# Part of the two down products of a macaron block computed by seven products of sums

## The chip, the cores and the metric

The kernel runs on one core of a Trainium2 chip. The metric is the device time of one execution in microseconds. Engines: TensorE (PE; PEld its weight load), VectorE (DVE), ScalarE (ACT), GpSimd (POOL), and SyncE (SP), whose queue issues loads. Matmuls accumulate into PSUM banks of 512 fp32 columns.

## What is computed

512 token rows of width 1024 pass through a feed-forward block, a token mixer (windowed attention and a gated recurrence), and a second feed-forward block. Each of the three has a residual with a factor and a layer norm behind it:

```python
def swiglu(x, w1, w3, w2):
    return (jax.nn.silu(x @ w1) * (x @ w3)) @ w2

x = layer_norm(DEEPNORM_ALPHA * x + 0.5 * swiglu(x, ffn1_w1[l], ffn1_w3[l], ffn1_w2[l]), ln1_g[l], ln1_b[l])
mix = token_mixer(x, ...)
x = layer_norm(DEEPNORM_ALPHA * x + mix, ln2_g[l], ln2_b[l])
x = layer_norm(DEEPNORM_ALPHA * x + 0.5 * swiglu(x, ffn2_w1[l], ffn2_w3[l], ffn2_w2[l]), ln3_g[l], ln3_b[l])
```

The hidden width is 2816, that is 22 feature tiles of 128. All is fp32.

## The kernel before

Every fp32 operand of a matmul is split into a high part (a cast to fp32r on ACT, line 74) and a low part (the difference, on DVE, line 75), by the helper `split`. A product is three matmuls: high by high, and the two mixed ones (lines 106 to 108). Weights come in blocks of 128 x 1024: SP's queue loads one into a raw buffer (`raw`, line 79, five buffers), and `wsplit` puts its two parts into a ring of four.

The up products of a feed-forward block already are done by seven products of sums of blocks (Strassen's scheme in Winograd's form) for all but the first pair of feature tiles: class `Quads`, whose matmuls are line 282 and whose sums of weights are line 297. Their operands, mixtures of the input's four blocks, lie in eight slots x0 to x7, named by `OPS` in the order in which the products use them. The gated results, g[0] to g[10], each a pair of feature tiles for all 512 tokens, stay in SBUF as g0 to g10; line 512 is the last multiplication that forms one.

The down product is `down_and_norm`. For each output half of 512 columns (dh = 0, 1) it goes through 22 feature tiles in eleven weight slabs; for every feature tile four row tiles of 128 tokens are multiplied, the last as two pieces of 256 columns. `lhs(k)` gives the two parts of a feature tile and splits them at first need, into the slots x0 to x7, into tiles of the pool `dn`, or into g4 and g5. The residual rows are loaded into g0 to g3 behind the first half's matmuls (`get_res`, line 549, on ACT's queue) and take the sums by `drain` (line 466). In the second half the last six feature tiles go row by row, so that the layer norm of a row tile runs beside the matmuls of the next.

The pool `up` (sums, gates) is closed before the pool `dn` is opened, and both lie on the same side of SBUF. The order of the instructions on each engine comes from a planner that runs when the kernel is built: it takes what is written first, but lets later instructions go ahead where it reckons that the earlier ones must wait. The class `Pipe` has the operands of a product prepared one product ahead in the order of writing.

Of the kernel before, what the change touches and what calls it, by code (L numbers as in the profile page):

```python
# [11 lines left out]
F32 = mybir.dt.float32  # L12
# [30 lines left out]
def body(ctx, tc, a):  # L43
# [400 lines left out]

    def down_and_norm(pool, lhs, nk, wsrc, get_res, scale, ln, done):

# [6 lines left out]
        stats = [pool.tile([P, 2 * n, 6], F32, name=f"st{t}", bufs=1) for t, n in enumerate(pieces)]  # L453
        ntail = min(6, nk - 2)
        res = None
        for dh in range(2):
# [6 lines left out]
            def drain(t, i):  # L463
                n = 512 // pieces[t]
                r_ = res[t][:, dh * 512 + i * n:dh * 512 + (i + 1) * n]
                nc.vector.scalar_tensor_tensor(out=r_, in0=r_, scalar=ALPHA / scale, in1=accs[t][i], op0=ALU.mult,
                                               op1=ALU.add)
                nc.vector.bn_stats(out=stats[t][:, dh * pieces[t] + i], in_=r_)

            def mul(t, i, k, h, l):  # L470
                n = 512 // pieces[t]
                c = slice(i * n, (i + 1) * n)
                tsl = slice(t * P, (t + 1) * P)
                gh, gl = lhs(k)
                mm3(accs[t][i], (gh[:, tsl], gl[:, tsl]), (h[:, c], l[:, c]), k == 0, k == nk - 1)

            for k0 in range(0, nk, 2):
                h, l = slab(wsrc[dh, k0 // 2])
                for k in (k0, k0 + 1):
                    c = (k - k0) * 512  # L480
                    item = (k, h[:, c:c + 512], l[:, c:c + 512])
                    if dh == 1 and k >= nk - ntail:
                        tail.append(item)
                        continue
                    for t, n in enumerate(pieces):
                        for i in range(n):
                            mul(t, i, *item)
            if dh == 0:
                res = get_res()
                for t, n in enumerate(pieces):  # L490
                    for i in range(n):
                        drain(t, i)
            else:
                for t, n in enumerate(pieces):
                    for i in range(n):
                        for item in tail:
                            mul(t, i, *item)
                        drain(t, i)
                    layer_norm_rows(pool, res[t], stats[t], g_bc, b_bc, LN_EPS / scale ** 2, n,
                                    lambda c: done(t, res[t], c))  # L500

    def ffn(x, stages, res_src, w13, w2, ln, done):
# [25 lines left out]
        with tc.tile_pool(name="dn", bufs=1, side="right") as dn:  # L528
            parts, pairs = {}, {}

            def lhs(k):
                p = k // 2
                if p not in parts:
                    if p < 8:
                        if p % 2 == 0:
                            pairs["hi"], pairs["lo"] = (slot(p + i, [P, 2, 2, S]) for i in range(2))
                        hi, lo = pairs["hi"][:, p % 2], pairs["lo"][:, p % 2]
                    elif p < 10:
                        hi, lo = (dn.tile([P, 2, S], F32R, name=f"g{n}{p}") for n in ("h", "l"))
                    else:  # L540
                        hi, lo = (big(i, dtype=F32R) for i in (4, 5))
# [9 lines left out]

            down_and_norm(dn, lhs, FT, w2, get_res, 0.5, ln, done)

# [594 lines left out]
    with tc.tile_pool(name="dn", bufs=1, side="right") as dn:  # L1148
        def get_res2():
            res = [big(t, [P, D]) for t in (4, 5, 10, 0)]  # L1150
            for t in range(TT):
                nc.scalar.dma_start(out=res[t], in_=x1_spill[:, t])
            return res

        down_and_norm(dn, lambda k: (mg[2 * (k // 4)][:, k % 4], mg[2 * (k // 4) + 1][:, k % 4]), KT, a["w_out"],
                      get_res2, 1.0, 2, next_x(x2_spill))
# [106 lines left out]
```

## Time and profile before

| | |
|---|---|
| median of 3 runs | 1267.06 us (1266.09 to 1267.49) |
| the profiled execution | 1268.93 us, its span 1267.1 us |
| first feed-forward: last up matmuls, down product, its last drains | 229 to 236 us, 229 to 360 us, 360 to 363 us |
| second feed-forward: last up matmuls, end of the down matmuls | 1130 to 1137 us, 1258 us |

The profile is of one execution. Times within it are microseconds from the start of its span. A matmul's own duration reaches beyond the start of the next, since matmuls are pipelined; how fast they follow each other is read from their starts. The same holds, by a little, for DVE and ACT.

### The profile page before, as it was taken

The numbers are of one execution on the slowest core, as the hardware profiler recorded it, in microseconds if no ns is written. First come the engines' busy times: TensorE is split into PE (matmuls) and PEld (weight loads), VectorE is DVE, ScalarE is ACT, GpSimd is POOL, SyncE is SP. The second block draws the span as 40 slices with busy tenths as digits, with TensorE's granted clock in tenths as the row PEclk, the third lists the DMA queues.
The fourth block names the chain that finished last, engine by engine and source line by source line (L and its number), as shares of the span: only waits on it lengthen the run. The fifth ranks groups of instructions, "written<-read, shape, count | busy, mean of one in ns | idle before, by whom it ended". The sixth has DMA issues, their size and how long they took to land.

```text
span 1267.1 us, 21689 instructions
## 1 busy us (share of the span) xinstructions
PE 1239.7 (98%) x9040; PEld 1168.6 (92%) x9040; DVE 929.1 (73%) x1304; ACT 628.5 (50%) x891; POOL 37.5 (3%) x37
## 2 busy tenths in 40 slices
PE   7999999999999999999999999999999999999997
PEld 7999999988899989989999998888899999998886
DVE  7987878723299999898778787464898778783325
ACT  5654555511146767678654765442365545562110
POOL 0000000000010000000001011000100000000001
PEclk9999999999999999999999999999999999999999
DMA  6423233532232335233223253653332332443211
GB/s 244 137 98 122 83 130 115 185 100 85 98 125 97 110 124 158 85 109 103 76 76 117 88 159 109 237 189 131 124 124 87 117 107 94 131 156 129 100 35 67
DMA packets 51139, 150.75 MB, mean 119 GB/s; under 512 B 5728, under 2 KB 12896, under 8 KB 51040
## 3 DMA queue, kind: packets, MB, share of 16 engines
q1 hardware_dynamic: 47008, 135.72, 32.9%
q10 hardware_dynamic: 4032, 13.63, 3.1%
q8 instruction: 71, 1.16, 0.4%
q14 instruction: 28, 0.23, 0.1%
HBM read 134.65 MB, written 14.68 MB: 118 GB/s over the span
## 4 chain that ended last, share of the span: by engine, by line
PE 86%; DVE 8%; issue 1%; POOL 1%; DMA 1%; ACT 1%; SPq 0%; DVEq 0%; POOLq 0%; ACTq 0%
PE A L282 50%; PE A L108 6%; PE A L107 6%; PE A L106 6%; PE B L107 4%; PE B L106 4%; PE B L108 4%; PE B L113 2%; DVE wlo L75 1%; PE B L991 1%; PE B L816 1%; POOL rstd L436 1%; DVE g L441 1%; DVE r L768 1%; PE B L763 1%
## 5 line engine op out<-in xcount | busy, mean ns | idle before, releaser
L282 PE MATMUL A<-x,whi 128*128 128x256 f32 x3840 | 546.1, 285 | 9.4 <-ACT whi L74 7.2
L282 PEld LDWEIGHTS A<-x,whi 128*128 128x128 f32 x3840 | 498.4, 193 | 11.6 <-ACT whi L74 7.7
L75 DVE TENSOR_TENSOR wlo<-raw,whi 128x1024 fp32r<-128x1024 f32 (+1 forms) x186 | 224.3, 1208 | 184.6 <-ACT whi L74 184.4
L74 ACT CAST whi<-raw 128x1024 fp32r<-128x1024 f32 (+1 forms) x186 | 192.9, 1041 | 316.2 <-PE A L108 129.0
L282 PE MATMUL A<-x,wlo 128*128 128x256 f32 x1920 | 312.4, 284 | 0.2 <-DVE wlo L75 0.2
L282 PEld LDWEIGHTS A<-x,wlo 128*128 128x128 f32 x1920 | 266.5, 193 | 0.9 <-issue 0.4
L74 ACT CAST whi<-wsum 128x1024 fp32r<-128x1024 f32 x128 | 134.5, 1051 | 136.5 <-PE A L282 96.6
L75 DVE TENSOR_TENSOR wlo<-wsum,whi 128x1024 fp32r<-128x1024 f32 x128 | 156.2, 1221 | 11.0 <-ACT whi L74 11.0
L106 PE MATMUL A<-whi,x 128*128 128x256 f32 (+1 forms) x360 | 115.5, 321 | 0.0
L107 PE MATMUL A<-wlo,x 128*128 128x256 f32 (+1 forms) x360 | 115.4, 321 | 0.0
L108 PE MATMUL A<-whi,x 128*128 128x256 f32 (+1 forms) x360 | 114.7, 319 | 0.0
L297 DVE TENSOR_TENSOR wsum<-raw 128x1024 f32<-128x1024 f32 x64 | 77.6, 1219 | 1.9 <-DMA raw<-in_w_fqg_dram 1.2
L297 DVE TENSOR_TENSOR wsum<-raw,wsum 128x1024 f32<-128x1024 f32 x64 | 78.1, 1221 | 0.8
L106 PEld LDWEIGHTS A<-whi,x 128*128 128x128 f32 x360 | 68.5, 190 | 5.1
L108 PEld LDWEIGHTS A<-whi,x 128*128 128x128 f32 x360 | 68.3, 190 | 4.9
L107 PEld LDWEIGHTS A<-wlo,x 128*128 128x128 f32 x360 | 68.4, 190 | 4.6
L107 PE MATMUL B<-wlo,x 128*128 128x512 f32 (+1 forms) x200 | 69.8, 349 | 0.0
L106 PE MATMUL B<-whi,x 128*128 128x512 f32 (+1 forms) x200 | 69.6, 348 | 0.0
L108 PE MATMUL B<-whi,x 128*128 128x512 f32 (+1 forms) x200 | 69.3, 347 | 0.0
L108 PE MATMUL A<-x,wlo 128*128 128x512 f32 (+1 forms) x160 | 59.9, 374 | 0.5 <-DVE wlo L75 0.5
L106 PE MATMUL A<-x,whi 128*128 128x512 f32 (+1 forms) x160 | 60.3, 377 | 0.0
L107 PE MATMUL A<-x,whi 128*128 128x512 f32 (+1 forms) x160 | 59.3, 371 | 0.0
(172 smaller groups left out, 1455.4 us busy)
## 6 DMA issues: line engine op xcount, KB each, us to landing
raw<-in_w_dram SPq DMA_DIRECT2D x130, 512.0 KB, 3.6
raw<-in_w_fqg_dram SPq DMA_DIRECT2D x24, 512.0 KB, 3.5
raw<-in_w_q_dram SPq DMA_DIRECT2D x8, 512.0 KB, 4.1
raw<-in_w_ga_dram SPq DMA_DIRECT2D x8, 512.0 KB, 3.3
raw<-in_w_gh_dram SPq DMA_DIRECT2D x8, 512.0 KB, 4.0
raw<-in_w_i_dram SPq DMA_DIRECT2D x8, 512.0 KB, 3.6
raw<-in_w_pa_dram SPq DMA_DIRECT2D x8, 512.0 KB, 4.5
g<-x_spill ACTq DMA_DIRECT2D x8, 512.0 KB, 4.6
```

The costliest lines, as they stand in the source:

```text
L74: nc.scalar.copy(out=hi, in_=src)
L75: nc.vector.tensor_tensor(out=lo, in0=src, in1=hi, op=ALU.subtract)
L106: nc.tensor.matmul(out, lhsT=lh, rhs=rh, start=first, stop=False, **kw)
L107: nc.tensor.matmul(out, lhsT=lh, rhs=rl, start=False, stop=False, **kw)
L108: nc.tensor.matmul(out, lhsT=ll, rhs=rh, start=False, stop=last, **kw)
L113: nc.tensor.transpose(out=tp[:, j * P:(j + 1) * P], in_=b, identity=ident)
L282: nc.tensor.matmul(reg, lhsT=w, rhs=x, start=first, stop=last, skip_group_check=True)
L297: nc.vector.tensor_tensor(out=t, in0=x, in1=y, op=ALU.add)
L436: nc.gpsimd.tensor_tensor(out=rstd, in0=ve, in1=pw, op=ALU.pow)
L441: nc.vector.scalar_tensor_tensor(out=r[:, c], in0=r[:, c], scalar=rstd, in1=b_bc[:, c], op0=ALU.mult, op1=ALU.add)
L763: nc.tensor.matmul(out, lhsT=qs[i][:, hf, qsl], rhs=k_hi[pp][:, hf, ksl], start=True, stop=False)
L768: nc.vector.tensor_tensor_reduce(out=neg[hf][:, i, :kb * P], in0=sc[hf][:, i * 256:i * 256 + kb * P], in1=amask[:, koff:], scale=-(HD ** - ...
```

## The change

The first eight feature tiles of each down product (g[0] to g[3]) no longer go through `down_and_norm`. A new function `seven`, called before it, splits the 512 tokens in two halves and the eight feature tiles in two halves of four, and the output columns are in two halves already: 2 x 2 blocks on each side. From them it forms four mixtures of the gated blocks (t1 to t4, in rooms g11, q0 and q1) and three plain ones (b11, b21, b22), puts their parts into slots x1 to x7, loads the residual rows, and runs seven products in a pipe, each as two halves h over the features. Weight sums are formed on DVE: p1 = w21 + w22 in q0, p3 = w11 + w21 in p0 and p1, p2 = w22 + p3 and later w12 + p2 in p2 and p3 (rooms; all in the pool `dn`). The products gather in six PSUM banks, and each bank is added to or taken from the residual rows, fourteen additions of 512 columns. `down_and_norm` then takes the fourteen other feature tiles, with the rows that `seven` returns, and its drain of the first half is a plain addition. The product of the mixer keeps its 8 tiles and its own rows.

```diff
--- before.py
+++ after.py
@@ -442,7 +442,8 @@
                                            op0=ALU.mult, op1=ALU.add)
             done(c)
 
-    def down_and_norm(pool, lhs, nk, wsrc, get_res, scale, ln, done):
+    def down_and_norm(pool, lhs, ks, wsrc, get_res, scale, ln, done, res=None):
+
 
 
         g_bc = pool.tile([P, D], F32, name="g_bc", bufs=1)
@@ -451,8 +452,8 @@
         nc.scalar.dma_start(out=b_bc, in_=a[f"ln{ln}_b"].broadcast_to([P, D]))
         pieces = [1] * (TT - 1) + [2]
         stats = [pool.tile([P, 2 * n, 6], F32, name=f"st{t}", bufs=1) for t, n in enumerate(pieces)]
-        ntail = min(6, nk - 2)
-        res = None
+        ntail = min(6, len(ks) - 2)
+        part = res is not None
         for dh in range(2):
 
             accs = [[bank("BA"[dh])] for _ in range(TT)]
@@ -463,8 +464,11 @@
             def drain(t, i):
                 n = 512 // pieces[t]
                 r_ = res[t][:, dh * 512 + i * n:dh * 512 + (i + 1) * n]
-                nc.vector.scalar_tensor_tensor(out=r_, in0=r_, scalar=ALPHA / scale, in1=accs[t][i], op0=ALU.mult,
-                                               op1=ALU.add)
+                if part:
+                    nc.vector.tensor_tensor(out=r_, in0=r_, in1=accs[t][i], op=ALU.add)
+                else:
+                    nc.vector.scalar_tensor_tensor(out=r_, in0=r_, scalar=ALPHA / scale, in1=accs[t][i],
+                                                   op0=ALU.mult, op1=ALU.add)
                 nc.vector.bn_stats(out=stats[t][:, dh * pieces[t] + i], in_=r_)
 
             def mul(t, i, k, h, l):
@@ -472,21 +476,21 @@
                 c = slice(i * n, (i + 1) * n)
                 tsl = slice(t * P, (t + 1) * P)
                 gh, gl = lhs(k)
-                mm3(accs[t][i], (gh[:, tsl], gl[:, tsl]), (h[:, c], l[:, c]), k == 0, k == nk - 1)
-
-            for k0 in range(0, nk, 2):
+                mm3(accs[t][i], (gh[:, tsl], gl[:, tsl]), (h[:, c], l[:, c]), k == ks[0], k == ks[-1])
+
+            for k0 in ks[::2]:
                 h, l = slab(wsrc[dh, k0 // 2])
                 for k in (k0, k0 + 1):
                     c = (k - k0) * 512
                     item = (k, h[:, c:c + 512], l[:, c:c + 512])
-                    if dh == 1 and k >= nk - ntail:
+                    if dh == 1 and k > ks[-1] - ntail:
                         tail.append(item)
                         continue
                     for t, n in enumerate(pieces):
                         for i in range(n):
                             mul(t, i, *item)
             if dh == 0:
-                res = get_res()
+                res = res or get_res()
                 for t, n in enumerate(pieces):
                     for i in range(n):
                         drain(t, i)
@@ -528,15 +532,18 @@
         with tc.tile_pool(name="dn", bufs=1, side="right") as dn:
             parts, pairs = {}, {}
 
+            def part(i):
+                return dn.tile([P, 2, S], F32R, name=f"p{i}")
+
             def lhs(k):
                 p = k // 2
                 if p not in parts:
                     if p < 8:
                         if p % 2 == 0:
-                            pairs["hi"], pairs["lo"] = (slot(p + i, [P, 2, 2, S]) for i in range(2))
+                            pairs["hi"], pairs["lo"] = (slot(p - 4 + i, [P, 2, 2, S]) for i in range(2))
                         hi, lo = pairs["hi"][:, p % 2], pairs["lo"][:, p % 2]
                     elif p < 10:
-                        hi, lo = (dn.tile([P, 2, S], F32R, name=f"g{n}{p}") for n in ("h", "l"))
+                        hi, lo = (part(2 * (p - 8) + i) for i in range(2))
                     else:
                         hi, lo = (big(i, dtype=F32R) for i in (4, 5))
                     split(hi, lo, g[p])
@@ -549,7 +556,115 @@
                     nc.scalar.dma_start(out=res[t], in_=res_src(t))
                 return res
 
-            down_and_norm(dn, lhs, FT, w2, get_res, 0.5, ln, done)
+            res = seven(dn, g, w2, get_res, ALPHA / 0.5)
+            down_and_norm(dn, lhs, range(8, FT), w2, None, 0.5, ln, done, res)
+
+    def seven(dn, g, w2, get_res, alpha):
+
+
+
+        op = {n: slot(i, [P, 2, 4, 256]) for i, n in enumerate(OPS) if n != "b12"}
+
+        def block(n, a):
+            return g[2 * int(n[1]) - 2 + a][:, :, (int(n[2]) - 1) * 256:int(n[2]) * 256]
+
+        def plain(n):
+            for a in range(2):
+                k = slice(2 * a, 2 * a + 2)
+                split(op[n][:, 0, k], op[n][:, 1, k], block(n, a))
+
+        def mixture(n, t, x, y):
+
+            for a in range(2):
+                k = slice(2 * a, 2 * a + 2)
+                if isinstance(x, str):
+                    nc.vector.tensor_tensor(out=t[:, k], in0=block(x, a), in1=block(y, a), op=ALU.subtract)
+                else:
+                    nc.vector.scalar_tensor_tensor(out=t[:, k], in0=x[:, k], scalar=-1.0, in1=block(y, a),
+                                                   op0=ALU.mult, op1=ALU.subtract)
+            split(op[n][:, 0], op[n][:, 1], t)
+
+        def tile_of(name, **kw):
+            return dn.tile([P, 1024], F32, name=name, **kw)
+
+        t1, t2, t4 = (t.rearrange("p (k c) -> p k c", k=4) for t in (big(11, [P, 1024]), tile_of("q0"), tile_of("q1")))
+        plain("b11")
+        mixture("t1", t1, "b11", "b12")
+        mixture("t2", t2, t1, "b22")
+        plain("b21")
+        mixture("t3", t1, "b22", "b12")
+        mixture("t4", t4, t2, "b21")
+        plain("b22")
+        res = get_res()
+
+        w11, p1, p2, p3 = {}, {}, {}, {}
+
+        def mul(bk, w, n, h, first, last):
+            wh, wl = w
+            for j in range(2):
+                js = slice(j * P, (j + 1) * P)
+
+                def mm(x, w, k, first=False, last=False):
+                    nc.tensor.matmul(bk[j], lhsT=op[n][:, x, 2 * h + k, js], rhs=w[:, k * 512:(k + 1) * 512],
+                                     start=first, stop=last, skip_group_check=True)
+
+                for k in range(2):
+                    mm(0, wh, k, first=first and h == 0 and k == 0)
+                    mm(1, wh, k)
+                for k in range(2):
+                    mm(0, wl, k, last=last and h == 1 and k == 1)
+
+        def add(bk, u, dh, sign=1, scale=None):
+
+            for j in range(2):
+                r = res[2 * u + j][:, dh * 512:(dh + 1) * 512]
+                o = ALU.add if sign > 0 else ALU.subtract
+                if scale:
+                    nc.vector.scalar_tensor_tensor(out=r, in0=r, scalar=scale, in1=bk[j], op0=ALU.mult, op1=o)
+                else:
+                    nc.vector.tensor_tensor(out=r, in0=r, in1=bk[j], op=o)
+
+        def plus(out, x, y):
+            nc.vector.tensor_tensor(out=out, in0=x, in1=y, op=ALU.add)
+
+        def g1(h):
+            w11[h] = raw(w2[0, h])
+            return wsplit(w11[h])
+
+        def g5(h):
+            w21, w22 = raw(w2[1, h]), raw(w2[1, 2 + h])
+            p1[h], p3[h], p2[h] = tile_of("q0"), tile_of(f"p{h}"), tile_of(f"p{2 + h}")
+            plus(p1[h], w21, w22)
+            w = wsplit(p1[h])
+            plus(p3[h], w11[h], w21)
+            plus(p2[h], w22, p3[h])
+            return w
+
+        def g2(h):
+            w12 = raw(w2[0, 2 + h])
+            w = wsplit(w12)
+            plus(p2[h], w12, p2[h])
+            return w
+
+        v, c, aa = ([bank(n) for _ in range(2)] for n in "AAB")
+        for prep, bk, n, first, last, adds in (
+                (g1, v, "b11", True, True, [(v, 0, 0, 1, alpha)]),
+                (g5, c, "t1", True, True, []),
+                (lambda h: wsplit(p2[h]), v, "t2", False, True, [(v, 1, 0, 1, alpha)]),
+                (g2, aa, "b21", True, True, [(aa, 0, 0)]),
+                (lambda h: wsplit(p3[h]), v, "t3", False, True, [(v, 1, 1, -1, alpha), (c, 1, 1, -1)]),
+                (lambda h: slab(w2[1, 2 + h]), v, "t4", False, True, [(v, 0, 1, -1, alpha)]),
+                (lambda h: wsplit(p2[h]), c, "b22", False, True, [(c, 1, 0)])):
+            for h in range(2):
+                def run(w, h=h, bk=bk, n=n, first=first, last=last, adds=adds):
+                    mul(bk, w, n, h, first, last)
+                    if h == 1:
+                        for x in adds:
+                            add(*x)
+
+                pipe.push(lambda prep=prep, h=h: prep(h), run)
+        pipe.pump()
+        return res
 
 
     mc = ctx.enter_context(tc.tile_pool(name="mc", bufs=1, side="right"))
@@ -1152,7 +1267,7 @@
                 nc.scalar.dma_start(out=res[t], in_=x1_spill[:, t])
             return res
 
-        down_and_norm(dn, lambda k: (mg[2 * (k // 4)][:, k % 4], mg[2 * (k // 4) + 1][:, k % 4]), KT, a["w_out"],
+        down_and_norm(dn, lambda k: (mg[2 * (k // 4)][:, k % 4], mg[2 * (k // 4) + 1][:, k % 4]), range(KT), a["w_out"],
                       get_res2, 1.0, 2, next_x(x2_spill))
 
 
```

## Rows read from the trace of the kernel before

**Rows 1.** The page, busy time: engine, us, share of the span, instructions.

```profile
PE 1239.7 (98%) x9040; PEld 1168.6 (92%) x9040; DVE 929.1 (73%) x1304; ACT 628.5 (50%) x891; POOL 37.5 (3%) x37
```

**Rows 2.** The page, chain that ended last, by engine.

```profile
PE 86%; DVE 8%; issue 1%; POOL 1%; DMA 1%; ACT 1%; SPq 0%; DVEq 0%; POOLq 0%; ACTq 0%
```

**Rows 3.** Busy time by stretch: us, engines' busy us (count), clock, DMA share, GB/s.

```profile
249.00:294.00 45.00, 45.00 (x243) 38.79 (x242) 9.80 (x8) 8.41 (x8) 0.00 (x0) 1.00 0.29 94
```

**Rows 4.** Timeline of PE, a slab: start us, us, engine, line, operation.

```profile
301.88 0.40 PE L106 MATMUL A<-whi,x 128*128 128x512 f32 x1
...
303.95 0.28 PE L106 MATMUL A<-whi,x 128*128 128x256 f32 x1
...
307.44 0.40 PE L106 MATMUL A<-whi,x 128*128 128x512 f32 x1
```

**Rows 5.** Groups by line: busy us, mean ns | idle before, releasers.

```profile
L74 ACT CAST whi<-wsum 128x1024 fp32r<-128x1024 f32 x128 | 134.5, 1051 | 136.5 <-PE A L282 96.6 <-issue 25.2 <-DVE wsum L297 9.0
...
L297 DVE TENSOR_TENSOR wsum<-raw,wsum 128x1024 f32<-128x1024 f32 x64 | 78.1, 1221 | 0.8
...
L466 DVE SCALAR_TENSOR_TENSOR g<-g,A 128x512 f32<-128x512 f32 x9 | 6.2, 684 | 12.4 <-PE A L108 12.4
```

**Rows 6.** Timeline of DVE, back to back.

```profile
226.03 1.22 DVE L75 TENSOR_TENSOR x<-g,x 128x1024 fp32r<-128x1024 f32 x1
227.16 0.68 DVE L367 TENSOR_TENSOR h<-m,A 128x512 f32<-128x512 f32 x1
227.76 1.22 DVE L75 TENSOR_TENSOR wlo<-raw,whi 128x1024 fp32r<-128x1024 f32 x1
```

**Rows 7.** Timeline of PE where up and down products meet.

```profile
229.24 0.40 PE L106 MATMUL B<-whi,x 128*128 128x512 f32 x1
...
230.63 1.12 PE L282 MATMUL A<-x,whi 128*128 128x256 f32 x8
...
236.38 0.40 PE L106 MATMUL B<-whi,x 128*128 128x512 f32 x1
```

**Rows 8.** Timelines of DVE and ACT's queue where a pool takes another's room.

```profile
238.37 0.69 DVE L512 SCALAR_TENSOR_TENSOR g<-c,h 128x512 f32<-128x512 f32 x1
239.09 0.33 ACTq L450 DMA_DIRECT2D g_bc<-in_ln_g_dram  x1
...
862.51 0.69 DVE L1136 TENSOR_TENSOR g<-g,r 128x512 f32<-128x512 f32 x1
863.29 0.34 ACTq L450 DMA_DIRECT2D g_bc<-in_ln_g_dram  x1
...
1138.95 0.69 DVE L512 SCALAR_TENSOR_TENSOR g<-c,h 128x512 f32<-128x512 f32 x1
1139.67 0.34 ACTq L450 DMA_DIRECT2D g_bc<-in_ln_g_dram  x1
```

**Rows 9.** DMA issues, 200 to 300 us: count, KB, us to landing.

```profile
raw<-in_w_dram SPq DMA_DIRECT2D x19, 512.0 KB, 3.4
g<-in_x_dram ACTq DMA_DIRECT2D x4, 512.0 KB, 3.9
...
b_bc<-in_ln_b_dram ACTq DMA_DIRECT2D x1, 512.0 KB, 6.2
```

**Rows 10.** Busy time by stretch, columns as in rows 3, at the end.

```profile
1262.00:1263.00 1.00, 0.00 (x0) 0.00 (x0) 1.00 (x3) 0.00 (x0) 0.55 (x1) 1.00 0.02 4
1263.00:1264.00 1.00, 0.00 (x0) 0.00 (x0) 1.00 (x2) 0.00 (x0) 0.00 (x0) 0.68 0.00 0
1264.00:1265.00 1.00, 0.00 (x0) 0.00 (x0) 0.13 (x1) 0.00 (x0) 0.00 (x0) 0.50 0.67 248
```

**Rows 11.** Timeline of PE: eight matmuls at the start, later, and the last.

```profile
10.02 1.91 PE L282 MATMUL A<-x,whi 128*128 128x256 f32 x8
...
14.68 1.12 PE L282 MATMUL A<-x,whi 128*128 128x256 f32 x8
...
1258.14 0.28 PE L108 MATMUL B<-whi,g 128*128 128x256 f32 x1
```

## What the change was predicted to do

> **What bounds the kernel now.** I read the page's busy shares first: TensorE is busy 98% of the span, VectorE (DVE) 73%, ScalarE (ACT) 50% [rows 1]. The chain that ended last is 86% TensorE [rows 2]. So a matmul taken away is worth its own length, as long as TensorE does not stop for something else. The share of DVE is a mean, so I read it by stage. In the plain down product it is low: 9.8 us of 45 us [rows 3]. The reader should see there that the down stage has a free DVE and a full TensorE, and that the change trades the second for the first. The question is whether the DVE work can be done in time at the place where it is put.
>
> **Part 1, matmuls removed.** A plain weight slab serves two feature tiles: eighteen 512-column matmuls and twelve 256-column ones. Its period is 307.44 - 301.88 = 5.56 us, and nine 512-column matmuls start within 303.95 - 301.88 = 2.07 us, 0.230 us each [rows 4]. Eight feature tiles in both output halves are eight slabs: 8 x 5.56 = 44.5 us. A product of sums has 2 halves x 2 row blocks x 6 = 24 matmuls of 512 columns; seven are 168, or 168 x 0.230 = 38.6 us. The saving is 5.9 us in each of the two feed-forward blocks. By itself that is 11.8 us.
>
> **Part 2, DVE work added.** A 1024-column difference or sum takes 1.22 us on DVE, a cast on ACT 1.05 us, and an addition from PSUM of 512 columns 0.68 us [rows 5]. Back to back the starts are 1.13 and 0.60 us apart [rows 6], and those are the prices that I add up. Operands: four mixtures of two subtractions (8 x 0.60 = 4.8), four low parts of 1024 (4.5) and three in halves (6 x 0.60 = 3.6). Weights: eight sums (9.0) and fourteen low parts (15.8). Results: fourteen additions (8.4). Together 46 us of DVE against 38.6 us of TensorE; before, the same features took 8 + 4 low parts, 13.6 us. The seven products can only run at full speed if several microseconds of this are done earlier.
>
> **Part 3, where the DVE work can start.** In the trace the planner does pull work of the down stage forward: the first down matmuls stand at 229.24, ahead of the last 48 up matmuls (two products, 230.63 to 236.38) [rows 7]. So the split of b11, t1 and its split, b21 and the first two weight slabs (the same DVE time as the four operand splits and slabs that they replace there) will also be done before the end of the up product, and I cost them at nothing; without that cover they would cost their 8 us. But t2, t4 and all weight sums (p1, p2, p3) are written into tiles of the pool dn, which takes the room of the pool up. What the trace shows of that: the first load into dn, g_bc, is issued at 239.09, just when the last DVE reader in up ends (238.37 + 0.69 = 239.06), although its data was free all along. In the other two places it is the same, 863.29 after 863.20 and 1139.67 after 1139.64 [rows 8]. I take it that nothing is written into dn before 239.1.
>
> **Part 4, the path from there.** The first product (b11) needs nothing of dn. Six of its 24 matmuls can take the gap at 229.24 that six down matmuls fill now; the other 18 follow at 236.4 and end at 236.4 + 18 x 0.230 = 240.5. The second product (t1) wants p1, whose room q0 holds t2 until t4 has been formed and t2 split. On DVE, in the order of the code: t2 (1.2) to 240.3, t3 (1.2) to 241.5, low part of t2 (1.13, its cast done meanwhile) to 242.6, t4 (1.2) to 243.8, low parts of t3 and t4 (2.3) to 246.1, p1 to 247.2; then the cast on ACT, 1.05, to 248.3. TensorE has nothing else: b21 needs a weight slab whose raw buffer (five in all) is held by the blocks that wait for p1 and p3, and the plain tiles come later in the same queue. **TensorE waits from 240.5 to 248.3, 7.8 us.** If p1 were taken as soon as t4 is formed (243.8) the wait would be 5.5; I take the order of the code, since these low parts are ready then.
>
> The same scarcity bites once more. p3 (to 248.4) frees the first raw buffer; only then is the sixth block loaded, 3.4 us to landing [rows 9], 251.8; sum 1.13 and cast 1.05 give 254.0. The first half of product t1 (12 x 0.230 = 2.8 us) ends at 251.1, so 2.9 us are lost, or about 1.3 if the first half of t2 fills in (p2 formed, cast and the PSUM bank of v drained by 251.9). This last needs the residual rows, which are now loaded before the products; they wait for t3 and then some 3.9 us [rows 9], about 246, so they hide behind the wait already there. Queued behind that addition on DVE would be the weight low parts. If loads land as late as the slowest of this stretch (6.2 us [rows 9]) 2.8 more are lost.
>
> The clock: after the last matmul (start 1258.14) the granted clock is still 1.00 in 1262 to 1263 and falls to a mean of 0.68 in the next microsecond and to 0.50 after it: from 2.4 to 1.2 GHz, some 4.9 us after TensorE went idle [rows 10, 11]. At the kernel's start eight matmuls take 1.91 us, later 1.12 [rows 11]. A wait of 7.8 us is longer than 4.9, so the first half of t1 probably runs at the low level: 5.5 us in place of 2.8, to 253.8. That still ends before the second weights are there (254.0), so the two losses overlap: 2.9 us for both, up to 2.8 more if the filling would otherwise have worked. The Trainium skill, "TensorE: Matmul & The Clock Gate", section "HAM oscillation — how this bites in real kernels", speaks against the change here: a burst of matmuls that follows an idle wait begins cold, and pays for it each time. No gap inside this kernel is long enough to show it, and rows 10 have it only at the end; by the rule my sum stays, without it the second loss would be 1.3 to 2.9.
>
> After that the list is easy: from 246.1 DVE has 8 sums, 12 low parts and 14 additions, 9.0 + 13.6 + 8.4 = 31 us, done by 277; TensorE has 248.3 + 6 x 5.5 + 2.9 = 284. DVE is ahead, and I put 0.6 us on additions that hold a bank (t4 follows t3 in the same two banks). What is behind the products (plain tiles, one split and one slab for 5.56 us) has slack, so the loss isn't won back. The plain additions in place of the scaled ones cost the same 0.68, at nothing.
>
> Sum for one block: 7.8 + 2.9 + 0.6 - 5.9 = +5.4 us; I add 0.5 for the in-order waits on landing residual rows, between 0 and 2: +5.9. Twice that is +11.8. The profiled execution took 1268.93 us around a span of 1267.1, 1.87 more than the median 1267.06; it becomes 1280.7, and on the median's scale **1279 us**. Ends: 5.5 + 1.3 - 5.9 = +0.9 a block (1269) and 7.8 + 2.9 + 2.8 + 2.8 + 1.6 - 5.9 = +12 a block (1291).
>
> **The rivals.** (a) *The room of dn is free piece by piece.* Then t2, t4 and the sums are formed during the last up products, where 8 us of DVE can be had, and TensorE doesn't stop at the seam: -5.9 + 1.5 for the second load and the banks, 1258 us. For it: the planner visibly pulls work forward [rows 7]. Against it: three releases of three at the last reader, and q0 is the first tile of dn, as g_bc was [rows 8]. It decides for the other side if the first dn write is earlier than about 234. With no stall at all it would be 1267.1 - 11.8 = 1255. The Trainium skill, "Perfetto Trace Analysis", section "Engine Utilization", says so: only TensorE has a ceiling that matters. The busy shares agree [rows 1], the seam does not. (b) *Another order on DVE.* t4 is taken before t3 and p1 before their low parts: p1 from 242.6, first matmul at 244.8, wait 4.3, second loss 1.3: -0.3 a block, no change, 1267. For: p1 then is ready; against: the code's order. (c) *DVE becomes the bound throughout*, if additions that wait for banks or rows hold the weight work behind them: the upper end and beyond, about 1290. Against: 31 us of work in 38 us.
>
> **How the numbers follow.** Forecast 0.68 (own range 1271 to 1287), (a) 0.14, of which 0.03 without any stall, (b) 0.10, (c) 0.08. The range 1266 to 1290 leaves out (a) and part of (c). A difference under 0.2% (2.5 us) can't be told from none. Faster: (a), 0.14. Same: most of (b), 0.08. Slower: the rest, 0.78.
>
> **What would show it.** Right: in each block a wait of TensorE of 6 to 9 us behind the 24 matmuls of the first product, ended by the cast of p1; the first DVE write into q0 right behind the last gate multiplication; a lower granted clock behind the wait; 168 product matmuls 0.23 us apart otherwise. Wrong: t2 formed while up matmuls still run, or the seam closed and the stage 5 us shorter.

## The result, and the profile after

The changed kernel takes 1284.81 us, the median of runs from 1283.84 to 1285.62 us; the kernel before, on the same chip, 1266.57 us (1265.06 to 1267.49). The ratio is 1.0141, with a 95% interval of 1.0127 to 1.0154: slower by 18.2 us. The forecast was 1279 us with a range of 1266 to 1290. The profiled execution took 1284.41 us around a span of 1282.6.

The page of the changed kernel, its busy times and its chain (they answer to [rows 1, 2]):

```profile
PE 1233.6 (96%) x8896; PEld 1156.1 (90%) x8896; DVE 995.2 (78%) x1388; ACT 647.6 (50%) x915; POOL 36.6 (3%) x37
...
PE 83%; DVE 11%; issue 2%; POOL 1%; DMA 1%; ACT 1%; SPq 0%; DVEq 0%; POOLq 0%; ACTq 0%
```

TensorE has 144 matmuls less and is busy 6 us less, and still the span grows by 15.5 us. So TensorE stands still for over 20 us that it was not idle before; the chain gives the difference to DVE (8 to 11%). The list of TensorE's waits says on what (us in total, times, longest; line 608 is the product's matmul, line 74 the cast of a high part on ACT, line 75 the subtraction of a low part on DVE):

```profile
PE A L608 <- ACT whi L74: 15.8, 2, 7.9
...
PE A L608 <- DVE wlo L75: 4.3, 2, 2.2
```

Each of the two waits stands once in each block. PE's timeline at the seam of the first block (start us, us, idle before in brackets) shows where:

```profile
228.40 1.09 PE L608 MATMUL A<-whi,x 128*128 128x512 f32 x4
...
239.26 0.61 PE L608 MATMUL A<-wlo,x 128*128 128x512 f32 x2
247.76 2.50 PE L608 MATMUL A<-whi,x 128*128 128x512 f32 x5 [7.88 <-ACT whi L74]
252.42 1.22 PE L608 MATMUL A<-wlo,x 128*128 128x512 f32 x2 [2.16 <-DVE wlo L75]
...
255.76 3.47 PE L608 MATMUL A<-whi,x 128*128 128x512 f32 x11
...
264.74 1.07 PE L608 MATMUL B<-whi,x 128*128 128x512 f32 x4
...
270.18 1.07 PE L608 MATMUL A<-whi,x 128*128 128x512 f32 x4
...
286.66 0.39 PE L106 MATMUL B<-whi,x 128*128 128x512 f32 x1
```

The first product (b11) runs to 239.9, six of its matmuls in the gap among the up matmuls (228.40), the rest from 235.60 on. Then TensorE waits 7.88 us for the cast of the sum p1 (the bracket in the line at 247.76). The first half of the second product (t1) comes in pieces, with a second wait of 2.16 us for the low part of the same p1; its second half begins only at 255.76. The plain matmuls begin at 286.66. DVE's timeline over the same stretch has the reasons:

```profile
237.67 0.68 DVE L516 SCALAR_TENSOR_TENSOR g<-c,h 128x512 f32<-128x512 f32 x1
238.38 1.29 DVE L583 SCALAR_TENSOR_TENSOR q<-g,g 128x512 f32<-128x512 f32 x2
...
244.28 1.22 DVE L628 TENSOR_TENSOR p<-raw 128x1024 f32<-128x1024 f32 x1
245.41 1.21 DVE L628 TENSOR_TENSOR q<-raw 128x1024 f32<-128x1024 f32 x1
246.55 1.22 DVE L75 TENSOR_TENSOR x<-q,x 128x1024 fp32r<-128x1024 f32 x1
247.68 1.21 DVE L628 TENSOR_TENSOR p<-raw,p 128x1024 f32<-128x1024 f32 x1
248.82 1.27 DVE L623 SCALAR_TENSOR_TENSOR g<-g,A 128x512 f32<-128x512 f32 x2
250.01 1.22 DVE L628 TENSOR_TENSOR p<-raw 128x1024 f32<-128x1024 f32 x1
251.15 1.21 DVE L75 TENSOR_TENSOR wlo<-q,whi 128x1024 fp32r<-128x1024 f32 x1
252.28 1.22 DVE L628 TENSOR_TENSOR p<-raw,p 128x1024 f32<-128x1024 f32 x1
253.42 1.22 DVE L628 TENSOR_TENSOR q<-raw 128x1024 f32<-128x1024 f32 x1
```

The cast of p1, on ACT's timeline:

```profile
246.66 1.04 ACT L74 CAST whi<-q 128x1024 fp32r<-128x1024 f32 x1 [1.23 <-DVE q L628]
```

The last gate multiplication of the up product (line 516) ends at 238.35, and the first write into the pool dn, the mixture t2 in tile q0, starts at 238.38. From there to 262 DVE never pauses. The forming of p1 (tile q0, line 628) begins at 245.41, behind t2, t3, t4, two of their low parts and a p3. Its low part could start when its cast has ended, at 247.70, but p2, two additions into the residual rows and a p3 stand in front of it in DVE's queue, so it starts at 251.15. The second half of p1 takes the same room q0, so it too comes behind that low part, and behind one more p2: 253.42.

Two accounts agree on the size. At full pace (the first matmul of one product at 264.74, that of the next at 270.18) 24 matmuls take 5.44 us, 0.2265 us each; 168 cost 38.05 us and the saving against [rows 4] is 44.5 - 38.05 = 6.45 us. The loss is 239.71 (the start of the last matmul of b11 and 0.2265 more) to 247.76, that is 8.05, then 8.0 us (to 255.76) for 12 matmuls worth 2.7, that is 5.3, and 30.9 us (to 286.66) for 132 matmuls worth 29.9, that is 1.0: together 14.35. Net +7.9 us a block. The other account goes by the first normalisation behind each down product, line 436 of POOL, in the kernel before (first block, second block, end):

```profile
347.21 1.43 POOL L436 TENSOR_TENSOR rstd<-ve,pw 128x1 f32<-128x1 f32 x1 [345.41 <-DVE ve L434]
895.84 1.30 POOL L436 TENSOR_TENSOR rstd<-ve,pw 128x1 f32<-128x1 f32 x1 [92.48 <-DVE ve L434]
1252.43 1.46 POOL L436 TENSOR_TENSOR rstd<-ve,pw 128x1 f32<-128x1 f32 x1 [3.22 <-DVE ve L434]
```

and after:

```profile
354.24 1.46 POOL L436 TENSOR_TENSOR rstd<-ve,pw 128x1 f32<-128x1 f32 x1 [109.35 <-DVE ve L434]
903.80 1.30 POOL L436 TENSOR_TENSOR rstd<-ve,pw 128x1 f32<-128x1 f32 x1 [93.35 <-DVE ve L434]
1267.80 1.46 POOL L436 TENSOR_TENSOR rstd<-ve,pw 128x1 f32<-128x1 f32 x1 [3.22 <-DVE ve L434]
```

They are 7.0, 8.0 and 15.4 us later: some 7 to 8 us for each block, and about 1 us for all that lies between. The profiled difference (15.5) is smaller than that of the medians (18.2) because the profiled execution of the kernel before was 2.4 us above its median here (1268.93 against 1266.57) and that of the changed kernel 0.4 below.

Of the clock, by stretches of 2 us (us, then busy time of PE, PEld, DVE, ACT, POOL; the number behind POOL's is the granted clock, then DMA share and GB/s):

```profile
242.00:244.00 2.00, 0.00 (x0) 0.00 (x0) 2.00 (x3) 0.00 (x0) 0.19 (x1) 0.90 1.00 379
...
254.00:256.00 2.00, 2.00 (x6) 1.09 (x5) 2.00 (x3) 1.33 (x2) 0.00 (x0) 0.50 0.93 313
256.00:258.00 2.00, 2.00 (x7) 1.59 (x8) 2.00 (x3) 2.00 (x3) 0.00 (x0) 0.68 0.93 330
258.00:260.00 2.00, 2.00 (x11) 1.65 (x10) 2.00 (x3) 1.62 (x2) 0.00 (x0) 1.00 0.41 166
```

It falls to the low level in the wait and is back at the high one a little after 257.

### The profile page after: what moved, and what is told of

It is laid out like the page before. It is cut to its first block, busy times and chain, and to the rows that moved or that the text cites. A ratio compares the mean times of both kernels' runs of the same rounds, so it can differ in the third digit from the quotient of the medians.

```text
span 1282.6 us, 21534 instructions
## 1 busy us (share of the span) xinstructions
PE 1233.6 (96%) x8896; PEld 1156.1 (90%) x8896; DVE 995.2 (78%) x1388; ACT 647.6 (50%) x915; POOL 36.6 (3%) x37
## 4 chain that ended last, share of the span: by engine, by line
PE 83%; DVE 11%; issue 2%; POOL 1%; DMA 1%; ACT 1%; SPq 0%; DVEq 0%; POOLq 0%; ACTq 0%
PE A L282 49%; PE A L108 5%; PE A L107 5%; PE A L106 5%; PE A L608 4%; PE B L107 2%; PE B L106 2%; PE B L108 2%; PE B L113 2%; DVE wlo L75 1%; PE B L1106 1%; PE B L931 1%; POOL rstd L436 1%; DVE g L441 1%; PE B L608 1%
## 5 line engine op out<-in xcount | busy, mean ns | idle before, releaser
L74 ACT CAST whi<-raw 128x1024 fp32r<-128x1024 f32 (+1 forms) x182 | 188.6, 1041 | 266.2 <-PE A L108 102.7
L75 DVE TENSOR_TENSOR wlo<-raw,whi 128x1024 fp32r<-128x1024 f32 (+1 forms) x182 | 219.3, 1207 | 125.9 <-ACT whi L74 125.7
L106 PE MATMUL A<-whi,x 128*128 128x256 f32 (+1 forms) x280 | 87.7, 313 | 0.0
L107 PE MATMUL A<-wlo,x 128*128 128x256 f32 (+1 forms) x280 | 87.5, 313 | 0.0
L108 PE MATMUL A<-whi,x 128*128 128x256 f32 (+1 forms) x280 | 87.0, 311 | 0.0
L608 PE MATMUL A<-whi,x 128*128 128x512 f32 x192 | 55.9, 418 | 15.9 <-ACT whi L74 15.8
L608 PEld LDWEIGHTS A<-whi,x 128*128 128x128 f32 x192 | 38.0, 202 | 26.5 <-ACT whi L74 18.2
L106 PEld LDWEIGHTS A<-whi,x 128*128 128x128 f32 x280 | 53.3, 191 | 3.0
L108 PEld LDWEIGHTS A<-whi,x 128*128 128x128 f32 x280 | 53.2, 190 | 2.9
L107 PEld LDWEIGHTS A<-wlo,x 128*128 128x128 f32 x280 | 53.3, 191 | 2.7
L74 ACT CAST x<-g 128x512 fp32r<-128x512 f32 (+1 forms) x57 | 42.2, 764 | 25.8 <-PE A L282 12.2
```

The costliest lines, as they stand in the source:

```text
L74: nc.scalar.copy(out=hi, in_=src)
L75: nc.vector.tensor_tensor(out=lo, in0=src, in1=hi, op=ALU.subtract)
L106: nc.tensor.matmul(out, lhsT=lh, rhs=rh, start=first, stop=False, **kw)
L107: nc.tensor.matmul(out, lhsT=lh, rhs=rl, start=False, stop=False, **kw)
L108: nc.tensor.matmul(out, lhsT=ll, rhs=rh, start=False, stop=last, **kw)
L608: nc.tensor.matmul(bk[j], lhsT=op[n][:, x, 2 * h + k, js], rhs=w[:, k * 512:(k + 1) * 512], start=first, stop=last, skip_group_check=True)
```

## The experiments

The theory: the loss is made at the seam by what DVE has to do before p1, and the reason is where the tiles lie (nothing is written into dn while up is read) and in which order DVE takes its work. The rivals: DVE is simply too slow for seven products; the clock makes the loss; one tile (q0) is to blame.

**e1: t2 and t4 formed in the up product's own rooms.** The operands of the products are made before the pool dn is opened; t2 and t4 take sum tiles of the up pool (the second added line stands ahead of the opening of dn). All else is as in the changed kernel.

```diff
-        t1, t2, t4 = (... for t in (big(11, [P, 1024]), tile_of("q0"), tile_of("q1")))
+        t1, t2, t4 = (... for t in (big(11, [P, 1024]), sum_room(), sum_room()))
...
+            early = seven_operands(g, q.sum_room, get_res, w2)
         with tc.tile_pool(name="dn", bufs=1, side="right") as dn:
```

> The changed kernel with one thing moved: t2 and t4 are written into the sum rooms of the pool up, which stand free after the last weight sum, and no longer into the pool dn. My theory (nothing is written into dn before the last reader of up, so that 7 us of operand work lie between that point and p1): t2, t4 and their low parts are formed before the up product ends, p1 starts at about 238.4 in place of 245.4, the wait of 7.9 us behind the first product falls to 1 us or less, some 3 us of later waits stay in each block, and each block is 3 to 4 us shorter than the plain one: 1260 us, 1257 to 1264. Rival 'DVE is the bound as such' (46 us of DVE work against 38 us of matmuls): the work only changes its place, the up products or the later products are held up instead, and the time stays over 1275.

Measured: 1274.09 us (1272.25 to 1278.76), ratio 1.0070 (1.0043 to 1.0097) to the kernel before. It won 10.7 us back, less than expected: the time lies 10 us above the range of the theory (1257 to 1264), and 1 us under the 1275 of the rival, so e1 alone does not decide between them. In its timeline of PE (its product is line 616) the second product follows the first at once, but the second half of t1 comes late:

```profile
241.60 1.98 PE L616 MATMUL A<-whi,x 128*128 128x512 f32 x8
244.20 1.20 PE L616 MATMUL A<-wlo,x 128*128 128x512 f32 x4 [0.63 <-DVE wlo L75]
250.18 4.16 PE L616 MATMUL A<-whi,x 128*128 128x512 f32 x11 [4.78 <-ACT whi L74]
```

and its timeline of DVE says why: p1's first half at 238.92, right behind the last gate, its second half only at 247.82, after an idle time that ends with a load.

```profile
238.92 1.23 DVE L636 TENSOR_TENSOR q<-raw 128x1024 f32<-128x1024 f32 x1
...
247.82 1.23 DVE L636 TENSOR_TENSOR q<-raw 128x1024 f32<-128x1024 f32 x1 [3.08 <-issue]
```

The first wait of 7.9 us is made by the rooms: with them moved it is gone. What is left is the scarcity of raw buffers. The sixth block can be loaded only when p3 (to 241.28) has read the first. Its load is issued at 241.36 and lands 6.4 us later, at 247.8, beside residual rows, g_bc and b_bc that are loaded in the same microseconds. I had reckoned 3.4 us for that load. That is 3.0 us of a miss of 5 to 7 us a block. Some 1.5 us more, by my estimate, is the clock: it was at 0.50 when the second half of t1 began, and the eleven matmuls from 250.18 to 254.18 took 4.0 us where 2.5 is the full pace. The rest I have not taken apart.

**e2: all of it moved.** As e1, and also both halves of p1 and the first p3 are formed ahead of dn, in two spare tiles of the up pool and one other free tile, and the first weight slabs are written ahead of t1. So rooms and the order of writing change together here.

```diff
+        def first_sum(h):
+            w21[h], w22[h] = raw(w2[1, h]), raw(w2[1, 2 + h])
+            p1[h] = spare(h)
+            nc.vector.tensor_tensor(out=p1[h], in0=w21[h], in1=w22[h], op=ALU.add)
+            early_w["t1", h] = wsplit(p1[h])
```

> As the run before, and besides both p1 sums in two spare rooms of up and the first p3 in g11 once t3 is formed, with the weight slabs of the first product written ahead of t1. So three of the eight sums, with their splits, lie before the end of the up product and the sixth raw buffer comes free some 8 us earlier. My theory: no wait of TensorE over 1 us at the seam, 168 matmuls at 0.227 us in place of eight slabs of 5.56, 6.4 us saved and at most 1 lost in each block: 1255 us, 1253 to 1259. Rival 'DVE is the bound': 1268 or more, with waits of up products on DVE.

Measured: 1260.60 us (1258.35 to 1264.26), ratio 0.9956 (0.9943 to 0.9968): by the medians 6.5 us faster than the kernel before on the same chip (1267.1), by the ratio 5.6, and 24 faster than the changed kernel. The rival (1268 or more) falls. The theory's range (1253 to 1259) is missed by 1.6 us: twice 2 us are lost where I had allowed 1. Its timeline of PE (product: line 631):

```profile
246.73 2.11 PE L631 MATMUL A<-whi,x 128*128 128x512 f32 x8 [0.34 <-ACT whi L74]
...
250.71 2.11 PE L631 MATMUL A<-whi,x 128*128 128x512 f32 x8 [0.95 <-ACT whi L74]
...
275.32 0.39 PE L106 MATMUL B<-whi,x 128*128 128x512 f32 x1
```

From the last up matmul (236.46) to the first plain one it takes 38.9 us for 163 matmuls worth 36.9; 1.3 of the 2 us lost are the two waits shown. So a block gains 6.45 - 2 = 4.5 us, twice that is 9.0, and the last normalisation of this execution (1243.44) is 9.0 us ahead of that of the kernel before. The medians give 6.5 of it; the profiled execution of the kernel before was 1.8 us above this chip's median. So DVE can feed seven products, though it was busy for 38.3 of these 38.9 us, and the work saved is real; what the change lost, it lost at the seam.

**e3: TensorE kept busy in the first wait.** 32 matmuls into a sum bank that nobody reads stand behind the first product.

```diff
+                    if n == "b11" and h == 1:
+                        spare = bank("B")
+                        for i in range(32):
+                            nc.tensor.matmul(spare, lhsT=op[n][:, 0, 0, :P], rhs=w[0][:, :512],
+                                             start=i == 0, stop=i == 31, skip_group_check=True)
```

> The changed kernel with 32 more matmuls of 512 columns behind the first product, into a spare bank that nobody reads (7.25 us at 0.227), so that TensorE is busy through most of the wait of 7.9 us. Theory: the clock has a share of its own, since granted 0.50 stands in the rows until about 257 while the p1 low part is there at 252.4; with the clock kept up the matmuls from 252.4 on run at 0.227 and 2.0 to 2.8 us are saved in each block: 1280 us, 1278.5 to 1281.5. Rival: the products behind the wait are held by DVE anyway, the clock costs nothing: 1284 to 1286.

Measured: 1286.02 us (1285.75 to 1287.14), ratio 1.0158 (1.0143 to 1.0173): nothing gained, a miss, and what the rival had (1284 to 1286). The clock only fell later; stretches of 2 us of this kernel:

```profile
254.00:256.00 2.00, 0.00 (x0) 0.00 (x0) 2.00 (x3) 1.09 (x2) 0.00 (x0) 0.53 0.94 350
256.00:258.00 2.00, 2.00 (x5) 1.61 (x6) 2.00 (x3) 2.00 (x3) 0.00 (x0) 0.50 0.87 299
```

The first half of t1 now ran at full speed, and TensorE waited the longer for the low part (2.52 us) and for the second half (2.15), which came at 256.00 as before. Whether the clock matters there stayed open; e7 takes it up.

**e4: the sums first.** p1 gets a room of its own (q2) and is written ahead of t2 and t4, with p3, p2 and the first weight slabs, still inside dn.

```diff
-            p1[h], p3[h], p2[h] = tile_of("q0"), tile_of(f"p{h}"), tile_of(f"p{2 + h}")
+            p1[h], p3[h], p2[h] = tile_of("q2"), tile_of(f"p{h}"), tile_of(f"p{2 + h}")
...
+        early["b11", 0], early["b11", 1] = g1(0), g1(1)
+        early["t1", 0] = g5(0)
         mixture("t1", t1, "b11", "b12")
```

> The changed kernel with p1 in a room of its own in dn, and with the first weight slabs and the whole first group of sums (p1, p3, p2 of the first half) written ahead of t2. Rival 'the room q0': p1 waits only because t2 holds its room; then p1 is there at 239.6, the first half of t1 starts at 240.8, the wait of 7.9 falls to 1 and stays away: 6 us less in each block, about 1272. My theory (all of it waits for dn, and DVE has the same work in front of it whichever comes first): the wait behind the first product falls to about 1 us, but one of 5 to 8 us stands behind the first half of t1, before t2 or the second half: 1281 to 1288.

Measured: 1287.12 us (1285.28 to 1288.22), ratio 1.0164 (1.0149 to 1.0179). The waits of TensorE on PE's timeline (product: line 627):

```profile
241.16 1.88 PE L627 MATMUL A<-whi,x 128*128 128x512 f32 x7 [0.87 <-ACT whi L74]
...
250.46 2.08 PE L627 MATMUL A<-whi,x 128*128 128x512 f32 x4 [6.07 <-ACT whi L74]
256.99 1.22 PE L627 MATMUL A<-wlo,x 128*128 128x512 f32 x2 [4.46 <-DVE wlo L75]
```

The first wait shrinks from 7.88 to 0.87 us, and two others take its place. DVE's first write into dn stands at 238.81, behind the last gate multiplication (to 238.77). The tile q0 is not to blame, and what is put first at the seam makes something else late as long as all of it starts there. That sinks the rival "q0".

**e5: only DVE's order.** As the changed kernel, but with edges between DVE's instructions: the low part of p1 and the second half of p1 come ahead of p2 and of the second p3; the additions and the splits of the plain tiles are held behind that low part (`gate_at[0]`).

```diff
+            with tc.issue_after(gate_at[0]):
+                at = nc.vector.tensor_tensor(out=p1[h], in0=w21, in1=w22, op=ALU.add).ins
+            with tc.issue_after(at):
+                w = wsplit(p1[h])
+                plus(p2[0], *kept[0])
+                plus(p3[h], w11[h], w21)
+                plus(p2[h], w22, p3[h])
```

> The changed kernel with nothing moved out of its rooms; only VectorE's order at the seam is set by hand: behind the low part of t4 come the low part of p1's first half, the two additions of the first product, and p1's second half, and only then the other sums (p2, p3 of the second half), which stood ahead of it. All the same work is done. Theory (the second loss of the changed kernel, 5.3 us between 247.76 and 255.76, is the place of two operations in VectorE's queue): the low part starts at 247.7 instead of 251.15, the wait of 2.16 us for it goes; p1's second half starts when its raw slab is there, at about 250.8 instead of 253.42, its cast ends at 252 to 253, and the second half of t1 starts at 253.1 instead of 255.76: 2.6 us a block, of which up to 1 us may be given back at the sum p2, so 1.6 to 2.6 us a block: 1279.5 to 1281.5 us. Rival (VectorE has 5 us too much work in front of the third product, and whatever is put ahead makes something else late): the waits move to the low part of p2 and the sum stays, 1283.5 to 1286 us. A second rival (the raw slab of p1's second half lands only near 253): the first wait of 2.16 goes, the second half still starts after 255: 1284 to 1285 us.

Measured: 1279.08 us (1277.38 to 1280.64), ratio 1.0101 (1.0084 to 1.0118), 5.7 us faster than the changed kernel: the theory, with a gain 0.4 us beyond its range (1279.5 to 1281.5). PE's timeline (product: line 609) and, behind it, DVE's:

```profile
246.90 2.07 PE L609 MATMUL A<-whi,x 128*128 128x512 f32 x4 [7.89 <-ACT whi L641]
...
252.80 2.81 PE L609 MATMUL A<-whi,x 128*128 128x512 f32 x11 [0.41 <-ACT whi L74]
...
282.91 0.39 PE L106 MATMUL B<-whi,x 128*128 128x512 f32 x1
```

```profile
246.88 1.23 DVE L642 TENSOR_TENSOR wlo<-q,whi 128x1024 fp32r<-128x1024 f32 x1
...
250.44 1.23 DVE L647 TENSOR_TENSOR q<-raw 128x1024 f32<-128x1024 f32 x1 [1.14 <-issue]
```

The first wait is untouched (7.89). From its end to the first plain matmul it is 36.0 us against 38.9 in the changed kernel: 2.9 us a block, 5.8 in two; the times show 5.7, or 5.2 when each kernel is set against the kernel before on its own chip. Of the 6.3 us that the changed kernel lost behind the first wait, 2.9 were the place of two operations in a queue. DVE now pauses 1.14 us for the load: the raw buffer is the next in line, as I had predicted, only that in the changed kernel it stood behind the queue.

**e6: the change in the first block alone.** The second block's down product is plain.

```diff
-            res = seven(dn, g, w2, get_res, ALPHA / 0.5)
-            down_and_norm(dn, lhs, range(8, FT), w2, None, 0.5, ln, done, res)
+            if ln == 1:
+                res = seven(dn, g, w2, get_res, ALPHA / 0.5)
+                down_and_norm(dn, lhs, range(8, FT), w2, None, 0.5, ln, done, res)
+            else:
+                down_and_norm(dn, lhs, range(FT), w2, get_res, 0.5, ln, done)
```

> Seven products in the first feed-forward block alone, the second block's down product plain as in the kernel before. Theory (each block pays for its own seam and nothing else is touched): block 1 costs +7.9 us between its seam and its first rstd, the mixer behind it +0.9 or nothing, block 2 nothing: 1266.6 + 8 to 9 = 1274.5 to 1276 us. Rival (the loss is carried from one block into the next, or the tighter store of the first block slows what follows): 1278 us or more. A rival from the other side (the second block pays most): 1270 us or less.

Measured: 1276.38 us (1275.51 to 1276.84), ratio 1.0079 (1.0064 to 1.0094) to the kernel before on the same chip (1266.01): +10.4 us, 0.4 above the expected range. With both blocks it was +18.2. So the blocks cost about the same, 10.4 and some 8; neither rival (1278 or more, 1270 or less) holds. The normalisation of the first block and the last one, on POOL's timeline:

```profile
354.61 1.46 POOL L436 TENSOR_TENSOR rstd<-ve,pw 128x1 f32<-128x1 f32 x1 [108.65 <-DVE ve L434]
...
1259.12 1.46 POOL L436 TENSOR_TENSOR rstd<-ve,pw 128x1 f32<-128x1 f32 x1 [3.22 <-DVE ve L434]
```

are 7.4 and 6.7 us behind those of the kernel before, and that of the second block (902.55) is 6.7 behind too: lost in the first block, carried to the end. That this is less than 10.4 comes from the executions that were profiled: that of the kernel before was 2.9 us above the median of this chip, that of e6 0.9 below its own.

**e7: TensorE busy through all the waits.** As e3, with 13 more idle matmuls between the high and the low part of t1's first half (`cold`) and 9 behind it.

```diff
+            if cold:
+                for j in range(2):
+                    for k in range(2):
+                        mm4(j, 0, wh, k, first=k == 0)
+                        mm4(j, 1, wh, k)
+                idle(13)
...
+                idle(9)
```

> The changed kernel with idle matmuls (into a sum bank that nobody reads, 512 columns each) in all three holes of the seam: 32 behind the first product, 13 between the high and the low part of t1's first half, 9 behind it, so that TensorE is busy from 239.7 to 256.2 us. The high and low parts of that half stand apart for it; nothing else is changed. If the clock falls because TensorE stands still, it now stays at 1.00 throughout. Theory (VectorE hands out the operands, the clock costs only the first matmuls behind 255.76): the second half of t1 starts at 256 as before, its 12 matmuls take 2.7 us instead of 3.5 to 4, the plain part starts 0.5 to 1 us earlier: 0 to 2 us in all, 1282.8 to 1285 us. Rival (the clock is what makes the second loss, and the falling operands only follow): the seam closes by 2 to 3 us a block, 1279 to 1281 us. If the clock falls in spite of the idle matmuls, it does not depend on standing still: 1284.8 us or more with 0.50 granted somewhere between 240 and 258 us.

Measured: 1285.99 us (1283.9 to 1286.83), ratio 1.0153 (1.0134 to 1.0172). The clock stays at 1.00 in every stretch from 240 to 264 us, as this one where it was 0.50 in the changed kernel, and the second half of t1 starts where it did:

```profile
254.00:256.00 2.00, 2.00 (x10) 1.37 (x8) 1.04 (x1) 0.93 (x1) 0.00 (x0) 1.00 0.96 393
```

```profile
248.04 2.12 PE L614 MATMUL A<-whi,x 128*128 128x512 f32 x8 [0.64 <-ACT whi L74]
...
256.17 1.19 PE L632 MATMUL A<-whi,x 128*128 128x512 f32 x4
...
277.55 1.17 PE L632 MATMUL A<-whi,x 128*128 128x512 f32 x4 [1.67 <-DVE g L647]
...
288.55 0.39 PE L106 MATMUL B<-whi,x 128*128 128x512 f32 x1
```

The wait of 1.67 us at 277.55 is the experiment's own: it is not in the changed kernel, and it is ended by additions out of a sum bank; the idle matmuls had taken a bank, and I read it as that. Without it the way from the first matmul of t1 to the first plain one is 288.55 - 248.04 - 1.67 = 38.84 us, against 38.90 in the changed kernel with its low clock. So the clock cost nothing in the changed kernel that DVE did not cost anyhow. The rival "clock" (1279 to 1281) falls. It is not free everywhere: in e3, where it was low from about 254 to 261, the way from the second half of t1 to the first plain matmul took 288.51 - 256.00 = 32.5 us, against 30.9 in the changed kernel. For e7 as a whole, the time is 1 us above the theory's range; with the 3.3 us of the two extra waits taken off it would be 1282.7, 0.1 below it.

## Why the prediction was right, and where it was off

**The matmuls removed.** Right: predicted 5.9 us a block, measured 6.45, since a product's matmuls come 0.2265 us apart and not 0.230. e2 shows that this saving reaches the end of the kernel when nothing stands in its way.

**The work on DVE.** Forecast 46 us a block; the page has 995.2 - 929.1 = 66.1 us more busy time for two blocks, beside 13.6 a block that fell away: 33.05 + 13.6 = 46.7. But the stage was fuller than the 31 us of work in 38 that I had counted: from 247.76 to 286.66 DVE was busy 37.8 of 38.9 us, since the planner put splits of the plain tiles and their slabs there too. That cost little: behind 255.76 TensorE lost 1.0 us.

**Where it can start.** Right, to the instruction: the first write into dn stands 0.03 us behind the last read of up. With it rival (a) fell for the kernel as it was changed. e2 is the case that (a) described, made by moving the tiles: 1260.60 against the 1258 that (a) was given. The price without any stall was 1255; the runs put the changed kernel 30 us above it, and the version with the seam closed 5.6 us above. The Trainium skill, "Perfetto Trace Analysis", section "Engine Utilization", says that "TensorE is the only engine with a meaningful compute ceiling". It says so of compute ceilings; that nothing stalls is not in it, as I had read it. The work that I costed at nothing (b11, t1, b21, the first slabs ahead of the seam) did cost nothing: no wait of TensorE stands in front of 239.9.

**The first wait.** Right: 7.8 us forecast from 240.5 to 248.3, measured 7.88 to 247.76, ended by the cast of p1, in both blocks. DVE took p3 and p1 ahead of t4's low part, an order between the one I took and rival (b)'s, so b's 4.3 us did not come. That the size fits to 0.1 us is in part luck: p3 stood where I had a low part of the same length, and both ends of the wait came 0.6 us earlier than forecast; e4 shows that an order of that kind only moves the wait.

**The second loss is the term that was mis-sized.** I put 2.9 + 0.6 + 0.5 = 4.0 us on all that comes behind the first wait; it measured 6.3. The 0.5 for residual rows did not come at all: DVE never paused for one. I had walked the path of the raw buffer (p3, load, p1's second half, cast, 254.0), and that chain is there: e1 and e5 both stop at it. But I had let the low part of p1 follow its cast at once. In the trace it starts 3.45 us after it, behind p2, two additions and a p3, and the second half of p1 cannot be written into q0 before it is done. So t1's second half began at 255.76 and not at 254.0, and behind that another 1.0 us was lost. e5 gives 2.9 us a block back by that order alone. With the saving, 0.55 better than forecast, and the first wait, 0.25 worse, the block comes to +7.9 in place of +5.9: 4 us in two, most of the 5.8 between 1279 and 1284.8. The rest is the 1 us between the blocks and the scatter of single executions.

**The clock.** Right as a forecast: it fell in the wait, the first half of t1 ran at 0.50, and it overlapped with the waits for operands. The Trainium skill ("TensorE: Matmul & The Clock Gate", section "HAM oscillation — how this bites in real kernels") says that a burst after an idle wait begins cold and pays each time. The trace agrees with the cold start (5 matmuls in 2.50 us); the payment was hidden here, as e7 shows. In e3 I had forgotten my own overlap and expected a gain from it.

**After that TensorE is the bound.** Right: 24 matmuls in 5.44 us, with DVE almost full beside it. Rival (c) fell with it.

## What to carry to other kernels

When work moves from the full engine to the free one, look at the first microseconds of the stage and not at the stage's mean: here DVE had time for all the work of the stage, and the loss came first of all from the 9 us that had to be done before the second product, none of which could start until a pool's last reader was done. Ask of each new tile whose room it takes, and until when that room is read; moving tiles into rooms that were already free, and writing the first sums and slabs earlier, turned +18 us into about -6. When an operand comes in two parts made by two engines, follow the later part through its engine's queue and not only through its data.

## What was not expected of the hardware

The clock did not fall at a fixed time after TensorE went idle. These are estimates: each 2-us stretch is taken as a mix of the two levels, 1.00 and 0.50. It fell 3.2 us after the end of the last matmul in e5 (0.55 in 242 to 244), 3.7 in the changed kernel (0.90 in 242 to 244) and 5.3 in e6 (0.56 in 246 to 248), where [rows 10] had 4.9 at the end of the kernel before. It came back 2.9 us after work resumed in e1 (0.72 in 252 to 254), 5.5 us in e5 (0.89 in 252 to 254), where TensorE then worked almost without a hole, and 9.5 us in the changed kernel (0.68 in 256 to 258), where holes lay between. In e3 it fell at 254.1 (0.53 in 254 to 256) although TensorE had worked for 1.2 us just before, between two holes of some 2 us.

Loads landed later where several queues loaded at once: the raw blocks of the seam had a median of 5.2 us and b_bc 7.2 us to landing from 236 to 262 us in the changed kernel, where [rows 9] had 3.4 and 6.2. In e1 the load that mattered took 6.4, and the share of the DMA engines stood near 1.00 around it. That the company is the reason was not tested.
